# A hybrid streaming encoder layer on one core: other durations in the table that sets the emission order

## The chip, the core and the metric

The kernel runs on one core of one Trainium2 chip. The metric is the device time of one execution in microseconds (us). TensorE is written PE, its weight loads PEld, VectorE DVE, ScalarE ACT, GpSimd POOL and SyncE SP. PE's granted clock stands in the profile as a share of full speed; its two levels are 2.4 and 1.2 GHz.

## The reference

One layer of a trunk is applied to a prompt of 1024 frames and to a sample of 32 frames with carried state, all in float32, width 1024. The kernel treats the two as one sequence of 1056 columns wherever it can.

```python
h = rmsnorm(x, ln_mix_g)
z = h @ w_in + b_in                       # 1024 -> 2952 columns, split among three head groups
y_a = mLSTM(q_a, k_a, v_a, i, f)          # 4 heads of 96, chunkwise recurrence, gated and normed
y_b = stick_breaking(q_b, k_b, v_b)       # 6 heads of 64, causal, a product scan along the keys
y_c = glu(s5(u))                          # 16 groups, diagonal complex state of 64
x = x + concat[y_a, y_b, y_c] @ w_out
x = x + cross_attn(rmsnorm(x), mem_k, mem_v, w_xq, w_xo)   # 4 heads of 256, 256 memory tokens
f = (silu(causal_conv3(h2 @ w_ffn_a)) * (h2 @ w_ffn_b)) @ w_ffn_down   # h2 = rmsnorm(x), width 2816
y = rmsnorm(x + f, ln_f_g)
```

The memory keys and values of the prompt (`rmsnorm(mem_prompt) @ w_xk`, `@ w_xv`), the new states and the keys and values of the layer are outputs as well.

## The kernel before

**Dense products.** Activations lie transposed (features on partitions, frames along the free axis). A float32 product is made of three products of a high and a low part: for each block of 128 features PE runs `w_hi*h_hi`, `w_hi*h_lo` and `w_lo*h_hi` into one PSUM bank of the pool `mm`. `WStream` reads 128 columns of a weight at a time (512 KB, two buffers `w_raw`), ACT rounds them into `w_hi`, DVE subtracts for `w_lo`. Frames go in three chunks: 384, 384 and 288 columns in the input projection, 352 each later. The feed-forward part works on blocks of 264 columns.

**Stages.** The main stream runs the input projection, the memory keys and values ("kv"), `w_out` for three chunks, `xq` and `xo` of the cross attention interleaved, the two feed-forward projections, `down`, and the last norm. Beside it run *sides*, Python generators that each emit one step and then yield: `s5` with `glu`, `stick` (48 units of 128 queries, each of score matmuls, two sigmoids on ACT, a scan on DVE, a product on DVE or, up to 512 keys, on POOL, transposes on PE, and the product with the values), `mlstm` (a prelude on the gates, then nine chunks), `head` of the cross attention, norms and loads. `mlstm` starts when `s5` and `glu` are done; its chunks start when the input projection is done; `w_out` for chunk 0 waits for `stick`, `s5` and the first mLSTM chunks.

**The planner.** The order in which instructions are emitted is worked out while the program is built, by a model inside the kernel. Every engine is wrapped in `Timed`; each call asks `cost` for a duration, `operands` for the time at which its operands are there (with the latencies `LAT` between engines and DMA), and `place` puts it on that engine's time line, into a gap of the last 15 us (`REORDER`) where it fits. The main stream's own clock `clk["pe"]` is the end of its last matmul. After every second feature block, that is after six matmuls, `group` pauses and `advance` lets each side emit its next step, if that step's inputs are ready by the planner:

```python
def run(self):                                  # Side.run, shortened
    if self.done or self.ready > clk["pe"]:
        return
    ...
        self.ready = chain[0] + 0.05 - self.slack
```

`until` raises `clk["pe"]` by 0.25 us at a time where the main stream has to wait for a side. DMAs are priced in `timed` itself, 0.5 us of issue, 0.65 us and bytes over 360 GB/s. Tiles in SBUF (`Mem`, `Bag`) and PSUM (`rot`: two banks `mm`, three `gp`, three `tp`) are handed out in the order of emission. The program that this gives goes to the tile framework with `schedule_with_timeline_sim=True`. All engine calls pass through one helper, so the profile shows one line (L173) for all of them, and instructions are told apart by tile names; `za`, `zb`, `zr`, `zf`, `zy` and so on are the large memory zones.

Of the kernel before, what the change touches and what calls it, by code (L numbers as in the profile page):

```python
# [7 lines left out]
F32 = mybir.dt.float32  # L8
# [45 lines left out]
def tile_fn(tc, *args):  # L54
# [33 lines left out]
    def width(x):  # L88
        n = 1
        for d in x.shape[1:]:  # L90
            n *= d
        return n
# [39 lines left out]
    class Timed:  # L132
# [3 lines left out]
        def cost(self, name, out, ins_, args, kw):  # L136
            n = width(out)
            if self.key == "pe":
                if name == "transpose":
                    return 0.003 + 0.000834 * n  # L140
                slow = args[2].dtype == F32
                return 0.003 + n * (0.001667 if slow else 0.000417)
            if self.key == "act":
                c = 0.1 + 0.00083 * n + 0.09 * (len(ins_) - 1)
                if tabs.get(args[2], tab[0]) != tab[0]:
                    tab[0] = tabs[args[2]]
                    c += 1.28
                return c
            if self.key == "pool":
                if kw.get("op") == ALU.pow:  # L150
                    return 0.3 + 0.165 * n
                return 0.15 + n * {"memset": 0.00084, "tensor_copy": 0.0033}.get(name, 0.0021)
            per = {"reciprocal": 0.0063, "tensor_scalar": 0.0007, "tensor_copy": 0.0009, "memset": 0.0009}.get(name, 0.00105)
            return 0.08 + per * (width(ins_[0]) if name == "tensor_reduce" else n)

        def __getattr__(self, name):
            f = getattr(self.eng, name)
# [2352 lines left out]
```

## Time and profile before

| | |
|---|---|
| median of 3 runs | 1724.47 us (1716.87 to 1728.94) |
| the profiled execution | 1717.52 us, of it a span of 1715.7 us |
| mean granted PE clock | 0.987 |
| PE busy | 1639.6 us (96%) |
| PEld busy | 1595.5 us (93%) |
| DVE busy | 1137.6 us (66%) |
| ACT busy | 754.9 us (44%) |
| POOL busy | 456.2 us (27%) |
| moved by DMA | 229.90 MB, mean 134 GB/s |

The span is the time from the first to the last instruction. Busy times count an engine's instructions alone. The ends of matmuls are modelled and overlap, so a single matmul's duration is longer than the distance from one to the next; the distance is read from a run of many.

### The profile page before, as it was taken

What the parts mean: (1) busy time and instruction counts of PE and PEld (TensorE: products, weight loads), DVE (VectorE), ACT (ScalarE), POOL (GpSimd) and SP (SyncE); (2) the same over time, 40 slices, a digit from 0 to 9 for tenths busy, and PEclk for the clock granted to TensorE, in tenths of its full rate; (3) what the DMA queues carried; (4) which work ended last, traced back from release to release, by engine and by line L of the source; (5) the groups of instructions that cost most, each with busy time, mean ns of one, the idle gap of its engine ahead of it and who ended that gap; (6) DMA issues with size and microseconds to landing.
All of it is one profiled execution on the core that took longest, in us unless ns stands there. A gap on an engine that the chain in (4) does not pass through costs nothing.

```text
span 1715.7 us, 30436 instructions
## 1 busy us (share of the span) xinstructions
PE 1639.6 (96%) x11616; PEld 1595.5 (93%) x11616; DVE 1137.6 (66%) x2221; ACT 754.9 (44%) x1480; POOL 456.2 (27%) x612
## 2 busy tenths in 40 slices
PE   5999999999999899999999889999999999999997
PEld 5999989998899799999998889999999998999997
DVE  6788878745786657766656678877777777233232
ACT  5434534634665554544444534444444445111143
POOL 5234425011213333201102554333333330000022
PEclk9999999999999999999999989999999999999999
DMA  7464544254579874456653555322222227332111
GB/s 216 145 179 109 128 109 106 77 157 136 142 231 268 235 226 136 139 160 183 182 162 112 156 156 160 98 88 81 75 76 75 76 74 259 96 100 75 45 67 65
DMA packets 328391, 229.90 MB, mean 134 GB/s; under 512 B 43564, under 2 KB 309707, under 8 KB 327991
## 3 DMA queue, kind: packets, MB, share of 16 engines
q1 hardware_dynamic: 309991, 214.57, 42.6%
q10 hardware_dynamic: 18256, 13.40, 2.7%
q8 instruction: 92, 1.51, 0.4%
q14 instruction: 52, 0.43, 0.1%
HBM read 170.95 MB, written 56.38 MB: 133 GB/s over the span
## 4 chain that ended last, share of the span: by engine, by line
PE 76%; DVE 9%; DMA 9%; ACT 2%; issue 2%; POOL 2%; SPq 1%; ACTq 0%; DVEq 0%; POOLq 0%
PE mm L173 47%; PE gp L173 19%; PE tp L173 10%; DVE zy L173 3%; DVE zf L173 2%; DVE zx L173 2%; DMA out_dram<-zf 2%; DVE zr L173 1%; DVE w_lo L173 1%; POOL zf L173 1%; DMA zf<-d_act 1%; SPq L173 1%; POOL zy L173 1%; DMA d_mv<-zr 1%; DMA zf<-d_e 1%
## 5 line engine op out<-in xcount | busy, mean ns | idle before, releaser
L173 PE MATMUL mm<-zb,w_hi 128*128 128x352 f32 (+4 forms) x1234 | 365.2, 329 | 2.7 <-DVE zb L173 1.3
L173 PE MATMUL mm<-zr,w_hi 128*128 128x352 f32 (+2 forms) x1358 | 289.9, 313 | 6.3 <-DVE zx L173 2.8
L173 ACT ACTIVATE w_hi<-w_raw 128x1024 fp32r<-128x1024 f32 (+1 forms) x150 | 149.6, 997 | 284.8 <-PE mm L173 203.8
L173 PE MATMUL mm<-zb,w_lo 128*128 128x384 f32 (+2 forms) x826 | 272.4, 330 | 0.0
L173 POOL TENSOR_TENSOR zf<-zf 128x352 f32<-128x352 f32 (+5 forms) x98 | 117.4, 1200 | 578.4 <-ACT zf L173 493.2
L173 PE MATMUL mm<-zr,w_lo 128*128 128x264 f32 (+2 forms) x1058 | 236.2, 304 | 0.7 <-ACT zf L173 0.7
L173 PEld LDWEIGHTS mm<-zb,w_hi 128*128 128x128 f32 x1234 | 226.4, 189 | 4.7 <-DVE zb L173 1.6
L173 PEld LDWEIGHTS mm<-zr,w_hi 128*128 128x128 f32 x1358 | 217.2, 192 | 8.3 <-DVE zx L173 3.1
L173 DVE TENSOR_TENSOR w_lo<-w_raw,w_hi 128x1024 fp32r<-128x1024 f32 (+1 forms) x127 | 160.4, 1263 | 54.9 <-ACT w_hi L173 54.2
L173 DVE TENSOR_TENSOR zx<-mm,zx 128x352 f32<-128x352 f32 (+3 forms) x120 | 62.7, 523 | 186.1 <-PE mm L173 184.3
L173 PE MATMUL mm<-za,w_hi 128*128 128x384 f32 (+1 forms) x552 | 183.1, 332 | 0.0
L173 PEld LDWEIGHTS mm<-zr,w_lo 128*128 128x128 f32 x1058 | 164.7, 189 | 0.9 <-ACT zf L173 0.9
L173 PEld LDWEIGHTS mm<-zb,w_lo 128*128 128x128 f32 x826 | 156.5, 190 | 0.7
L173 PE MATMUL tp<-ident,zf 128*128 128x128 f32 (+3 forms) x530 | 89.2, 286 | 28.6 <-DVE zf L173 20.6
L173 PE MATMUL mm<-zy,w_hi 128*128 128x352 f32 x456 | 113.1, 324 | 1.6 <-DVE zx L173 1.6
L173 PE MATMUL gp<-zy 128*128 128x132 f32 (+13 forms) x722 | 109.8, 290 | 3.1 <-DVE zg L173 2.4
L173 DVE TENSOR_TENSOR zy<-zy 128x16 f32<-128x16 f32 (+9 forms) x371 | 97.3, 303 | 16.3 <-POOL zy L173 7.7
L173 ACT ACTIVATE zf<-gp 128x512 f32<-128x512 f32 (+6 forms) x180 | 75.6, 476 | 73.9 <-PE gp L173 57.1
L173 PEld LDWEIGHTS mm<-za,w_hi 128*128 128x128 f32 x552 | 105.6, 191 | 0.5
L173 PEld LDWEIGHTS gp<-zy 128*128 128x128 f32 (+6 forms) x722 | 97.3, 186 | 5.4 <-DVE zg L173 2.6
L173 PEld LDWEIGHTS tp<-ident,zf 128*128 128x128 f32 (+3 forms) x530 | 64.7, 146 | 38.2 <-DVE zf L173 19.2
L173 POOL TENSOR_TENSOR zy<-zy 128x16 f32<-128x16 f32 (+8 forms) x123 | 82.5, 682 | 64.4 <-DVE zy L173 54.6
(232 smaller groups left out, 3358.7 us busy)
## 6 DMA issues: line engine op xcount, KB each, us to landing
w_raw<-in_w_ffn_a_dram SPq DMA_DIRECT2D x27, 512.0 KB
w_raw<-in_w_out_dram SPq DMA_DIRECT2D x24, 512.0 KB
w_raw<-in_w_xq_dram SPq DMA_DIRECT2D x24, 512.0 KB
w_raw<-in_w_xo_dram SPq DMA_DIRECT2D x24, 512.0 KB
w_raw<-in_w_in_dram SPq DMA_DIRECT2D x23, 512.0 KB
d_act<-zx SPq DMA_DIRECT2D x22, 528.0 KB
zf<-d_act SPq DMA_DIRECT2D x22, 528.0 KB
w_raw<-in_w_ffn_down_dram SPq DMA_DIRECT2D x16, 512.0 KB
```

Source lines behind the costliest of these rows:

```text
L173: return f(*args, **kw)
```

## The change

Only the function `cost` is edited, which gives the planner its durations in us (`n` is the number of elements along the free axis). A float32r or bfloat16 matmul goes from 0.003 + 0.000417n to 0.013 + 0.000417n with a floor of 0.109, a float32 one likewise with a floor of 0.216. An ACT instruction goes from 0.1 + 0.00083n, and 0.09 for each operand beyond the first, to 0.17 + 0.00087n, and 0.19 where it also accumulates. The fixed part of a DVE instruction goes from 0.08 to 0.15, a scan doubles per element, and a copy takes the general 0.00105 in place of 0.0009. PE transposes, POOL, DMA, the latencies, the slacks and the pauses stay. The instructions are the same; the order in which they are emitted, and with it which buffer each takes, follows from the new numbers.

```diff
             if self.key == "pe":
                 if name == "transpose":
                     return 0.003 + 0.000834 * n
-                slow = args[2].dtype == F32
-                return 0.003 + n * (0.001667 if slow else 0.000417)
+                if args[2].dtype == F32:
+                    return max(0.216, 0.013 + n * 0.001667)
+                return max(0.109, 0.013 + n * 0.000417)
             if self.key == "act":
-                c = 0.1 + 0.00083 * n + 0.09 * (len(ins_) - 1)
+                c = 0.17 + 0.00087 * n + (0.19 if "accum_out" in kw else 0.0)
                 if tabs.get(args[2], tab[0]) != tab[0]:
                     tab[0] = tabs[args[2]]
                     c += 1.28
...
-            per = {"reciprocal": 0.0063, "tensor_scalar": 0.0007, "tensor_copy": 0.0009, "memset": 0.0009}.get(name, 0.00105)
-            return 0.08 + per * (width(ins_[0]) if name == "tensor_reduce" else n)
+            per = {"reciprocal": 0.0063, "tensor_scalar": 0.0007, "memset": 0.0009,
+                   "tensor_tensor_scan": 0.0021}.get(name, 0.00105)
+            return 0.15 + per * (width(ins_[0]) if name == "tensor_reduce" else n)
```

## Rows read from the trace of the kernel before

**Rows 1.** The page: busy times, and the span in 40 slices.

```profile
PE 1639.6 (96%) x11616; PEld 1595.5 (93%) x11616; DVE 1137.6 (66%) x2221; ACT 754.9 (44%) x1480; POOL 456.2 (27%) x612
...
PE   5999999999999899999999889999999999999997
...
PEclk9999999999999999999999989999999999999999
```

**Rows 2.** Busy time of each engine by stretch, clock, DMA share, GB/s.

```profile
50.00:401.00 351.00, 344.24 (x2353) 329.14 (x2352) 267.15 (x706) 156.67 (x322) 108.61 (x211) 1.00 0.48 129
401.00:475.00 74.00, 67.02 (x448) 60.62 (x447) 51.22 (x76) 45.53 (x90) 15.71 (x25) 0.95 0.55 152
475.00:594.00 119.00, 110.00 (x900) 105.35 (x899) 88.50 (x168) 71.48 (x201) 33.61 (x37) 0.95 0.87 245
594.00:650.00 56.00, 50.85 (x337) 48.74 (x338) 35.61 (x53) 30.02 (x64) 20.47 (x14) 1.00 0.70 211
650.00:930.00 280.00, 279.32 (x1819) 272.47 (x1819) 179.71 (x394) 128.88 (x258) 41.77 (x33) 1.00 0.52 156
930.00:1100.00 170.00, 153.58 (x1158) 150.50 (x1157) 134.45 (x215) 76.27 (x138) 83.64 (x79) 0.97 0.48 147
1100.00:1400.00 300.00, 300.00 (x2468) 300.00 (x2467) 231.07 (x384) 127.23 (x235) 101.54 (x133) 1.00 0.26 77
1400.00:1700.00 300.00, 295.89 (x1912) 293.70 (x1912) 117.33 (x177) 86.78 (x119) 26.33 (x30) 0.99 0.31 99
```

**Rows 3.** PE's waits from 50 to 1100 us: total us, times, longest.

```profile
PE gp L173 <- ACT w_hi L173: 6.6, 1, 6.6
PE tp L173 <- DVE zf L173: 6.6, 5, 2.9
PE tp L173 <- ACT zf L173: 4.3, 2, 2.2
PE tp L173 <- POOL zf L173: 3.6, 2, 2.0
...
PE gp L173 <- DVE zr L173: 0.5, 1, 0.5
PE mm L173 <- ACT zr L173: 0.2, 1, 0.2
```

**Rows 4.** Chain of waits in order of time: start, us, what.

```profile
543.14 5.76 DMA out_dram<-zf
...
719.98 3.87 PE mm L173 x24
...
1098.13 2.92 PE tp L173 x24
```

**Rows 5.** DVE groups by form: count, busy us, mean ns, idle before.

```profile
L173 DVE TENSOR_TENSOR zr<-tp,zr 128x512 fp32r<-128x512 f32 x40 | 26.8, 679 | 4.3 <-ACT zr L173 4.2
...
L173 DVE TENSOR_TENSOR zy<-zy 128x16 f32<-128x16 f32 x161 | 22.7, 182 | 2.8 <-POOL zy L173 1.4 <-ACT zy L173 0.6
...
L173 DVE TENSOR_TENSOR_SCAN zf<-zf 128x1024 f32<-128x1024 f32 x6 | 13.7, 2282 | 1.0 <-ACT zf L173 1.0
```

**Rows 6.** ACT groups by form.

```profile
L173 ACT ACTIVATE w_hi<-w_raw 128x1024 fp32r<-128x1024 f32 x127 | 134.6, 1060 | 240.1 <-PE mm L173 187.0 <-issue 30.5 <-DMA w_raw<-in_w_out_dram 7.7
L173 ACT ACTIVATE zf<-gp 128x512 f32<-128x512 f32 x72 | 39.7, 609 | 12.4 <-PE gp L173 8.9 <-POOL zf L173 2.3 <-DMA d_ys<-zy 1.0
```

**Rows 7.** DVE's largest group from 64 to 465 us, forms merged.

```profile
L173 DVE TENSOR_TENSOR zy<-zy 128x16 f32<-128x16 f32 (+9 forms) x333 | 88.9, 309 | 9.8 <-PE tp L173 3.0 <-ACT zy L173 2.7 <-POOL zy L173 2.2
```

**Rows 8.** PE in order of time: mLSTM prelude's last transpose, input projection's last matmul.

```profile
456.13 0.20 PE L173 MATMUL tp<-ident,zy 4*96 4x4 f32 x1
...
464.94 0.29 PE L173 MATMUL mm<-zb,w_lo 128*128 128x288 f32 x1
```

**Rows 9.** Waits of SP's DMA queue from 475 to 594 us.

```profile
SPq L173 <- DVE zf L173: 31.3, 14, 10.8
```

## The prediction

> **What bounds the kernel now.** I read the page's busy times and slices first [rows 1]: PE is busy 96% of the span, DVE 66%, ACT 44%, and PE's slices stand at 8 or 9 but for the first and the last. No instruction is added or removed, so the change can win only time in which PE does nothing, or runs slowly. The table of stretches says where that is [rows 2]. From 650 to 930, 1100 to 1400 and 1400 to 1700 us PE idles 0.7, 0.0 and 4.1 us: 880 us, half of the span, have nothing to give. The rest idles 351.0 - 344.2 = 6.8, then 7.0, 9.0 and 5.1 us up to 650 (end of the input projection, the kv stage, the first `w_out`), and 16.4 us from 930 to 1100 (the change to the feed-forward part). With 0.7 us between 650 and 930 that makes 45 us. The granted clock is below full in three of these stretches, 0.95 over 74 and 119 us and 0.97 over 170 us: (74 + 119) x 0.05 + 170 x 0.03 = 14.8 us more. The ceiling of any reordering is thus near 60 us, 3.5%; start and end of the span, where inputs come in and results go out, are left as they are.
>
> Then PE's waits between 50 and 1100 us [rows 3], which total 44.4 us. Ten kinds end with DVE (6.6 us down to 0.5, the last shown), 19.6 us; five end with ACT other than on `w_hi` (4.3 down to 0.2), 9.7 us. These 29.3 us depend on the durations that the table corrects. The single wait of 6.6 us on `w_hi` is the first half of a weight sum of the feed-forward part: a load, two POOL sums and a rounding that the code emits at a fixed point of the main stream; it stays. POOL ends 5.9 us, a DMA 1.8 and issue 0.8; their prices stay.
>
> **The change part by part.** What counts is not a price but its ratio to the main stream's clock: a side's step is emitted at the first pause at which `clk["pe"]` has passed its ready time.
>
> *The main stream.* 24 matmuls of 352 columns take 3.87 us, 161 ns each, 24 of 264 take 2.92 us, 122 ns [rows 4]. The old table says 149.8 and 113.1 ns, the new 159.8 and 123.1. So one pause (six matmuls) is 0.90 us in the old plan, 0.96 in the new, 0.97 on the chip. A table whose matmuls alone grew would only emit every step earlier; the sides' prices grow with it.
>
> The Trainium skill has a rule that speaks against this part: its page "TensorE: Matmul & The Clock Gate", section "Back-to-back issue gap", gives N/2.4 + 2.5 ns from one warm matmul to the next, 149.2 ns for 352 columns, which is the old price. The trace disagrees, with 161 ns. By the page the new table would put the main stream 7% too slow and sides too early against it, and I would put the whole change at no gain; by the row it is a correction, and the sum below stands.
>
> *An ordinary step: one ACT and one DVE instruction of 512.* Old 0.525 + 0.618 = 1.14 us, new 0.615 + 0.688 = 1.30, measured 0.609 + 0.679 = 1.29 [rows 5, 6]. In pauses: 1.27, 1.36, 1.33. A step that moves by 0.09 of a pause is emitted at another pause in one case of eleven. The rounding of a weight, 1024 wide, goes from 0.95 to 1.06 (measured 1.06) but is tied to the main stream's tiles and moves nowhere. Of the 22.7 us of waits beyond the stick's transposes, one eleventh is 2 us, and its sign is open since banks and buffers then go to other takers. I take 0; bounds a third of it either way, -7 to +7.
>
> *The stick's scans.* The scan over 1024 is priced 1.16 us before, 2.30 after, and takes 2.28 [rows 5]: from 1.3 pauses to 2.4. This is the one large error that goes. Its victims are the transposes that follow scan and product: PE waits 6.6 us in 5 waits of `tp` for DVE's `zf`, and 3.6 us in 2 for POOL's, whose product stands behind the same scan [rows 3]. Emitted a pause later, these transposes find their operand and six main matmuls run in between. Two thirds of 10.2 us, since POOL's own price stays short: -7. Bounds 0 and -10.2.
>
> *Small DVE steps in `s5`.* 161 instructions of 16 elements take 182 ns, priced 97 before and 167 after [rows 5]. `s5` with `glu` and the mLSTM prelude is a chain of such steps, and the prelude's last transpose comes 8.8 us before the last matmul of the input projection [rows 8]. Such steps and wider ones of `zy` on `zy`, nearly all of that chain, are 333 between 64 and 465 us [rows 7]: 333 x 0.07 = 23 us of price; with its copies, scans and ACT I estimate the chain 23 to 40 us longer in the plan. The main stream beside it, these 401 us, gets 7% longer, 28 us. The chain slips by -5 to +12 us against it. Only what exceeds the cover of 8.8 us reaches the mLSTM chunks: 0, at most +3 us; then the kv matmuls are next in line.
>
> *What is moved past queues.* Stores and loads of a step go with it on SP. DMA and POOL prices are unchanged while the main stream's grow 7%, so steps that wait for a load come up to 7% earlier against the matmuls: a load of 4 us, a quarter of a pause. In most of the span DMA has room (0.25 to 0.55 busy) and I cost that at nothing; the kv stage at 0.87 and 245 GB/s has none [rows 2], and there it is the second rival, 0 to +24 us.
>
> *Clock.* Idle and lowered clock fall into the same stretches, so I charge 14.8 us in proportion to the 44.4 us of waits: 7/44.4 x 14.8 = 2.3, taken as -2; bounds -10 and +5.
>
> Sum: 0 - 7 + 0 + 0 - 2 = -9 us, from 1717.5 of the profiled execution to 1708.5. That execution is 7.0 us below the median of the runs; carried over, the median goes from 1724.5 to 1715.5, half a per cent, below what a measurement of this kernel can tell from no change (about 1%, 17 us: its three runs alone span 12).
>
> **The rivals.** (a) *The order is repaired all over.* With DVE and ACT right, half to all of the 29.3 us of waits go, with their share of the clock (29.3/44.4 x 14.8 = 9.8): -20 to -39, the middle 1695 us. For it: these waits are just those that too early a transpose makes. Against: an ordinary step hardly moves, and the kv stage's waits for ACT `zf` stand behind stores that take 5.76 us each [rows 4], which no price of ACT mends.
>
> (b) *SP's queue in the kv stage.* SP issues in order; a store that waits for its DVE copy holds back the weight load behind it. In 119 us SP already waits 31.3 us in 14 waits for DVE's `zf`, 2.2 us each [rows 9]. Steps fed by loads now come earlier against the main stream, and their stores with them. The stage has 16 weight tiles of 512 KB; if each comes half such a wait later than PE wants it, that is 16 x 1.12 = 18 us and 6 us of clock, +24: 1748 us. It decides once the waits use up the lead of the second `w_raw` buffer, one tile of 24 matmuls, some 3 us; the longest is already 10.8. Against: none of PE's waits in this stage is on a weight; the one of 6.6 us comes after 930 us.
>
> (c) *The order hardly changes on the engines.* Emission is not yet an engine's queue: the framework's scheduler sorts once more, and ready main matmuls fill in for a late transpose either way. Then nothing moves: 1724 us. For it: PE already loses only 6.8 us from 50 to 401 us, where most of the stick and all of `s5` run under the wrong prices.
>
> **How the numbers follow.** The forecast gets 0.50, (a) 0.15, (b) 0.20, (c) 0.15. Faster by over 1% means under 1707: all of (a) and a fifth of the forecast, where its bounds reach low, 0.25. Slower by over 1%, above 1742: nine tenths of (b), 0.18. Within 1%: 0.57. The range goes from 1692 (the forecast's bounds summed, -27 and a little of the runs' spread; it also takes in the middle of (a)) to 1748 (b); the lower part of (a) and what lies beyond (b) stay out.
>
> **What would show it.** Right: fewer and shorter waits of `tp` for `zf` on DVE and POOL between 100 and 510 us, the same dense stretches, PE idle from 401 to 650 us at some 15 in place of 21 us. (a) would show a clock of 1.00 in the kv stage; (b) waits of PE for `w_hi` or `w_lo` between 475 and 594 us and a longer kv stage; (c) the same waits with the same totals. The forecast fails if a buffer goes to another taker and a stage starts late, most likely where `w_out` waits for three sides at once, or if `s5` slips past the input projection by more than its cover.

## The result and the profile after

The changed kernel takes 1770.41 us (median of 4 runs, 1765.79 to 1775.45) where the kernel before, timed beside it, takes 1721.12: a ratio of 1.0288, 95% interval 1.0259 to 1.0318. It is slower by 49 us, outside the predicted range of 1692 to 1748. The profiled executions, 1771.12 and 1717.52 us, differ by 53.6.

The page after, the lines of [rows 1]:

```profile
PE 1672.3 (95%) x11616; PEld 1622.8 (92%) x11616; DVE 1137.3 (64%) x2221; ACT 755.5 (43%) x1478; POOL 444.4 (25%) x612
...
PE   5999999999889798999999879999999998999998
...
PEclk9999999998889797999999999999999999999999
```

DVE works 1137.3 us against 1137.6 before, ACT 755.5 against 754.9: the same work. What differs stands in slices 10 to 16 of the PE clock, some 400 to 710 us.

By stretches, as [rows 2], with the same borders up to 650 us and the later ones moved by 54:

```profile
50.00:401.00 351.00, 339.52 (x2297) 324.37 (x2296) 262.45 (x690) 154.25 (x313) 102.14 (x203) 0.99 0.48 130
401.00:475.00 74.00, 73.07 (x463) 65.71 (x461) 41.00 (x69) 33.22 (x72) 10.82 (x24) 0.93 0.35 99
475.00:594.00 119.00, 102.79 (x770) 96.87 (x771) 83.66 (x135) 71.96 (x158) 22.58 (x30) 0.87 0.78 224
594.00:650.00 56.00, 48.59 (x300) 45.81 (x298) 29.06 (x60) 24.73 (x79) 18.80 (x21) 0.79 0.58 141
650.00:760.00 110.00, 99.27 (x580) 95.79 (x579) 67.82 (x109) 48.69 (x96) 30.77 (x28) 0.89 0.57 161
760.00:984.00 224.00, 223.99 (x1474) 217.59 (x1473) 138.76 (x335) 98.99 (x212) 23.96 (x18) 1.00 0.54 162
984.00:1154.00 170.00, 151.39 (x1136) 148.44 (x1137) 133.92 (x212) 77.26 (x139) 83.22 (x79) 0.96 0.47 144
1154.00:1454.00 300.00, 300.00 (x2469) 300.00 (x2468) 231.19 (x385) 127.01 (x235) 101.24 (x132) 1.00 0.26 77
```

From 760 us on the stretches are those of before [rows 2], 54 us later. The wait on `w_hi` in the feed-forward part marks it exactly. PE in order of time, before and then after:

```profile
1000.48 0.59 PE L173 MATMUL gp<-zr,w_hi 128*128 128x264 f32 x1 [6.65 <-ACT w_hi L173]
```

```profile
1054.68 0.59 PE L175 MATMUL gp<-zr,w_hi 128*128 128x264 f32 x1 [6.64 <-ACT w_hi L175]
```

From there to the end of the span it is 715.2 us before and 714.6 after. The last result of `w_out` is added by DVE at 702.22 us before and at 754.04 after:

```profile
702.22 0.53 DVE L173 TENSOR_TENSOR zx<-mm,zx 128x352 f32<-128x352 f32 x1 [1.33 <-PE mm L173]
```

```profile
754.04 0.53 DVE L175 TENSOR_TENSOR zx<-mm,zx 128x352 f32<-128x352 f32 x1 [0.48 <-PE mm L175]
```

That is 52 of the 54 us. The input projection ends 4 us late (below), so some 48 us of the loss lie between its end and the end of `w_out`. In the traces of all the runs below, what follows the last result of `w_out` takes 1010 to 1015 us, so no run loses anything behind it.

Between 401 and 760 us PE idles 0.9 + 16.2 + 7.4 + 10.7 = 35 us after; before, 7.0 + 9.0 + 5.1 in the first three stretches [rows 2] and nothing from 650 to 760, 21 us. The larger part is the clock. These 359 us before and after:

```profile
401.00:760.00 359.00, 337.87 (x2391) 324.57 (x2391) 249.68 (x431) 200.65 (x448) 89.61 (x93) 0.97 0.66 190
```

```profile
401.00:760.00 359.00, 323.72 (x2108) 304.19 (x2107) 221.54 (x371) 178.60 (x402) 82.98 (x100) 0.88 0.59 166
```

The clock takes (1 - 0.88) x 359 = 43 us after and 11 before, 32 more, against 14 us more of idle time. Over the whole span it is (1 - 0.966) x 1769.3 = 60 us after and (1 - 0.987) x 1715.7 = 22 before.

What came late is the mLSTM. The two rows of [rows 8] after:

```profile
469.22 0.30 PE L175 MATMUL mm<-zb,w_lo 128*128 128x288 f32 x1
...
546.84 0.21 PE L175 MATMUL tp<-ident,zy 4*96 4x4 f32 x1
```

The input projection ends 4 us later than before (464.94), the mLSTM prelude 91 us later (456.13). Its nine chunks then run for the most part behind the kv stage, whose last matmul starts at 585 us, with no other dense work beside them than `w_out`. The chain of waits after, in that part (start, us, what):

```profile
579.91 5.81 DMA d_ya<-zy
585.78 2.65 DMA zy<-d_uu
...
607.31 5.74 DMA d_ya<-zy
...
629.80 4.06 DMA d_ya<-zy
633.92 5.78 DMA zy<-d_uu
...
652.63 3.60 DMA d_ya<-zy
656.25 7.03 DMA zy<-d_uu
```

A chunk stores its result (`d_ya`) from the buffer into which a later chunk then loads its decay rows (`d_uu`); there are three such buffers. The chain runs through these stores and loads, which take some 35 of its 140 us between 550 and 690 us. The length of the nine chunks is not fixed by them: from the first score matmul to the last state product it is 112 us before, 129 after, and between 94 (e3) and 141 (e11) in the runs below. `w_out` for its chunks 1 and 2 waits for all nine. From its last result for chunk 0 to its first for chunk 1 it is 5 us before and 20 after:

```profile
635.28 0.51 DVE L173 TENSOR_TENSOR zx<-mm,zx 128x352 f32<-128x352 f32 x1
640.02 0.52 DVE L173 TENSOR_TENSOR zx<-mm,zx 128x352 f32<-128x352 f32 x1 [0.22 <-PE mm L173]
```

```profile
669.96 0.52 DVE L175 TENSOR_TENSOR zx<-mm,zx 128x352 f32<-128x352 f32 x1
689.78 0.52 DVE L175 TENSOR_TENSOR zx<-mm,zx 128x352 f32<-128x352 f32 x1
```

### The profile page after: what moved, and what is told of

Its sections match the earlier page's. It is cut to its first block, busy times and chain, and to the rows that moved or that the text cites. A ratio compares the mean times of both kernels' runs of the same rounds, so it can differ in the third digit from the quotient of the medians.

```text
span 1769.3 us, 30471 instructions
## 1 busy us (share of the span) xinstructions
PE 1672.3 (95%) x11616; PEld 1622.8 (92%) x11616; DVE 1137.3 (64%) x2221; ACT 755.5 (43%) x1478; POOL 444.4 (25%) x612
## 4 chain that ended last, share of the span: by engine, by line
PE 75%; DMA 10%; DVE 8%; ACT 3%; issue 2%; POOL 1%; SPq 0%; DVEq 0%; POOLq 0%; ACTq 0%
PE mm L175 47%; PE gp L175 18%; PE tp L175 9%; DVE zy L175 3%; DVE zf L175 2%; DVE zx L175 2%; DMA d_ya<-zy 1%; DVE zr L175 1%; DMA zy<-d_uu 1%; ACT zy L175 1%; DMA w_raw<-in_w_out_dram 1%; POOL zy L175 1%; DMA zf<-d_act 1%; DVE w_lo L175 1%; POOL zf L175 1%
## 5 line engine op out<-in xcount | busy, mean ns | idle before, releaser
L175 PE MATMUL mm<-zb,w_hi 128*128 128x352 f32 (+3 forms) x1298 | 387.7, 334 | 5.2 <-DVE zb L175 2.4
L175 PE MATMUL mm<-zr,w_hi 128*128 128x352 f32 (+2 forms) x1294 | 276.8, 315 | 12.8 <-ACT zr L175 4.8
L175 PE MATMUL mm<-zb,w_lo 128*128 128x384 f32 (+4 forms) x858 | 283.4, 330 | 0.0
L175 PEld LDWEIGHTS mm<-zb,w_hi 128*128 128x128 f32 x1298 | 241.6, 192 | 9.7 <-DVE zb L175 3.6
L175 PEld LDWEIGHTS mm<-zr,w_hi 128*128 128x128 f32 x1294 | 207.6, 193 | 15.3 <-ACT zr L175 5.4
L175 PEld LDWEIGHTS mm<-zb,w_lo 128*128 128x128 f32 x858 | 163.9, 191 | 0.7
L175 PE MATMUL tp<-ident,zf 128*128 128x128 f32 (+5 forms) x566 | 94.6, 287 | 25.2 <-DVE zf L175 14.6
L175 PEld LDWEIGHTS tp<-ident,zf 128*128 128x128 f32 (+5 forms) x566 | 69.3, 148 | 35.4 <-DVE zf L175 13.4
L175 PE MATMUL gp<-zy 128*128 128x132 f32 (+9 forms) x586 | 92.6, 296 | 0.8 <-ACT zf L175 0.7
L175 PEld LDWEIGHTS mm<-zy,w_hi 128*128 128x128 f32 x456 | 80.8, 191 | 5.1 <-ACT zr L175 4.6
```

The lines of the kernel that those rows point to most:

```text
L175: return f(*args, **kw)
```

## The experiments

Sixteen kernels, each timed in three rounds beside the kernel before; what a run loses is counted against the kernel before as it was timed beside that run. The table has for each the ratio, and from its trace, in us from the span's start: the last PE instruction of the mLSTM prelude, the last matmul of the input projection, the last of the kv stage, and the last state product of the mLSTM chunks (the row of matmuls `128*96 128x97`).

```
run                     median  ratio  95% interval      prelude input kv  chunks
before                                                       456   465 578  605
after                   1770.4  1.0288 1.0259-1.0318         547   469 585  680
e1_prelude_held         1747.3  1.0168 1.0141-1.0195         531   463 564  648
e2_dve_prices_alone     1764.2  1.0262 1.0243-1.0280         560   458 563  669
e3_pe_act_prices_alone  1763.7  1.0259 1.0239-1.0280         444   483 633  639
e4_s5_slack_1           1737.2  1.0101 1.0084-1.0119         486   462 596  623
e5_pe_prices_alone      1741.9  1.0122 1.0091-1.0153         429   478 602  619
e6_act_prices_alone     1736.7  1.0082 1.0061-1.0102         484   474 592  621
e7_dve_tenth            1742.8  1.0124 1.0093-1.0155         468   478 602  633
e8_pe_percent           1734.9  1.0067 1.0048-1.0086         479   478 590  609
e9_after_dve_157        1749.3  1.0143 1.0109-1.0177         526   474 586  654
e10_after_act_177       1746.8  1.0124 1.0092-1.0156         530   480 594  646
e11_after_dve_143       1766.0  1.0250 1.0217-1.0284         545   471 584  681
e12_pe_percent_held     1749.4  1.0142 1.0109-1.0175         530   471 564  652
e13_scan_price_alone    1731.1  1.0066 1.0049-1.0083         474   472 585  610
e14_dve_fixed_alone     1733.0  1.0078 1.0061-1.0095         511   467 582  637
e15_new_table_tuned_a   1743.0  1.0131 1.0116-1.0146         507   477 591  642
e16_new_table_tuned_b   1740.3  1.0116 1.0093-1.0140         512   468 601  633
```

The first four test theory L (the late prelude is the loss) against rivals Q (SP's queue, rival (b) of the prediction) and S (any reshuffle loses).

**e1, the prelude alone held**, with the old table:

```diff
-            while "gate" not in avail or not s5_done:
+            while "gate" not in avail or not s5_done or not h_free:
```

> The kernel before with its old table; the mLSTM prelude alone is held until the input projection is done (one more condition in the while of its first step). Theory L (the loss is the late mLSTM prelude: its last transpose came 91 us later after the change, 547 against 456 us, and the median 49 us, 0.55 us per us of slip): the prelude starts at some 465 us instead of 401 and ends at 510 to 525, a slip of 55 to 70 us, so 1750 to 1760 us. Rival Q (SP's queue and DMA-fed steps that come early against a dearer main stream): the table is old, no change, 1715 to 1730. Rival S (any reshuffled order loses what the slacks were chosen for): some loss, but the three w_out chunks need not be where it lies; 1735 to 1760.

Measured 1747.3, +28 us, 3 us under L's range and inside S's; the prelude ended at 531. Q, which expected no change, missed. The stretch from the kv stage to `w_out`, here before, after, and e1, shows how much PE got done in the same 285 us (the count after the busy time):

```profile
475.00:760.00 285.00, 270.85 (x1944) 263.95 (x1944) 198.47 (x356) 155.12 (x359) 73.90 (x68) 0.98 0.69 199
```

```profile
475.00:760.00 285.00, 250.65 (x1645) 238.47 (x1646) 180.54 (x303) 145.38 (x331) 72.16 (x77) 0.86 0.66 184
```

```profile
475.00:760.00 285.00, 252.88 (x1779) 244.56 (x1778) 181.92 (x324) 142.19 (x337) 66.94 (x75) 0.92 0.67 187
```

1944 matmuls before, 1645 after, 1779 with nothing but the prelude held; the clock falls with them, 0.98, 0.86, 0.92.

**e2, the DVE prices alone** (the last part of the change on the old table).

> The kernel before with the new DVE prices alone; PE and ACT prices are old. Theory L: the s5 chain is DVE's, its price grows and the main stream's does not, so the prelude ends at least as late as after the change, 540 us or later, and the time is 1765 to 1785 us. Rival Q (the PE price decides): 1715 to 1730. Rival S: 1735 to 1770.

Measured 1764.2, +45 us, the prelude at 560, 102 us behind the input projection. That is a microsecond under L's range and inside S's. The price of PE is old here, so Q falls as the whole cause.

**e3, PE and ACT prices alone** (the first two parts of the change).

> The changed kernel with the old DVE prices back; PE and ACT prices are new. Theory L: the main stream is dearer, s5 hardly, so the prelude ends before the input projection does, earlier than the 456 us of before, and the time is 1710 to 1730 us. Rival Q: the PE price stays, so does the loss, 1760 to 1775. Rival S: 1735 to 1770.

Measured 1763.7, though the prelude ended at 444, well ahead. L as the whole cause fell here; the ranges of Q and S both held this value.

**e4, the changed kernel with more slack for `s5` and `glu`:**

```diff
-SLACK = [-0.25, 1, -0.5]
+SLACK = [1, 1, -0.5]
```

> The changed kernel with the slack of s5 and glu at 1 in place of -0.25, so that each of their steps is emitted up to 1.25 us earlier against the main stream. Theory L: the prelude's last transpose comes at 480 to 500 us, a slip of 25 to 45 us against before, and 15 to 25 us of loss remain, 1735 to 1747 us. Rival Q: nothing on SP's queue is mended, 1760 to 1775. Rival S: any value from 1730 to 1780, without regard to where the prelude ends.

Measured 1737.2, 18 us over the kernel before, the prelude at 486: 31 of the 49 us come back, as L had it; S allowed any value. The stretch of e4:

```profile
475.00:760.00 285.00, 263.42 (x1892) 255.87 (x1892) 196.58 (x353) 159.58 (x373) 76.66 (x77) 0.96 0.68 192
```

1892 of 1944 matmuls are back, and the clock is at 0.96.

The next four split e3 and test S by neighbours: kernels with a price moved by so little that nothing is corrected.

**e5 and e6, the PE prices alone and the ACT prices alone.**

> The kernel before with the new PE prices alone. The run with PE and ACT prices lost 44 us although its prelude came early, so theory L (late prelude) is not the whole. Theory M (a dearer main stream by itself stretches the stages from the input projection to w_out: sides are emitted too early against it): 1750 to 1770 us. Theory L: 1715 to 1730. Theory S (any other order loses, since the order of before was picked among many by its measured time): 1730 to 1770, without a reason in the stages.

> The kernel before with the new ACT prices alone. Theory L: the prelude slips by 20 to 25 us against before and 5 to 15 us are lost, 1725 to 1735. Theory M: the main stream's price is old, 1715 to 1725. Theory S: 1730 to 1760.

1741.9 and 1736.7: each costs, PE's less than M asked for, ACT's 2 us more than L had, both inside S's ranges. Together (e3) they cost more than the sum, 44 us against 20 + 15.

**e7 and e8, two neutral neighbours of the kernel before:**

```diff
-            return 0.08 + per * (width(ins_[0]) if name == "tensor_reduce" else n)
+            return 0.087 + per * (width(ins_[0]) if name == "tensor_reduce" else n)
```

```diff
-                return 0.003 + n * (0.001667 if slow else 0.000417)
+                return 0.003 + n * (0.001667 if slow else 0.000421)
```

> The kernel before with the fixed part of a DVE instruction at 0.087 in place of 0.08, a tenth of the change and no correction worth the name. Theories L and M: the prelude and the main stream stay where they were, so 1715 to 1728 us. Theory S: another order, and 10 to 30 us lost, 1730 to 1750.

> The kernel before with the price of a float32r column at 0.000421 in place of 0.000417, one per cent. Theories L and M: 1715 to 1728 us. Theory S: 10 to 30 us lost, 1730 to 1750.

1742.8 and 1734.9: 21 and 13 us lost by changes that correct nothing. S holds for this part: the order of before is better than orders next to it.

**e9, e10, e11, three neutral neighbours of the changed kernel** (0.157 for DVE's 0.15, 0.177 for ACT's 0.17, 0.143 for DVE's 0.15), **and e12, e8 with the prelude held** as in e1.

> The changed kernel with the fixed part of a DVE instruction at 0.157 in place of 0.15: a neutral neighbour of the changed kernel, as two runs before were neighbours of the old one, which lost 13 and 21 us against it. Theory S+ (both kernels are draws: the old one a picked good one, its neighbours 1735 to 1743; the changed one a plain draw of a table that is no better and no worse): 1730 to 1755 us, on the average of the neighbours near 1742. Theory L+ (what is left above the old neighbours, some 30 us, is the late prelude, which the new table always brings): 1755 to 1780.

> The changed kernel with the fixed part of an ACT instruction at 0.177 in place of 0.17, a second neutral neighbour. Theory S+: 1730 to 1755 us. Theory L+: 1755 to 1780.

> The changed kernel with the fixed part of a DVE instruction at 0.143 in place of 0.15, a third neutral neighbour; of the three its mLSTM prelude is emitted latest against the end of the input projection, near to where the changed kernel has it. Theory S+: 1730 to 1755 us, no later than the other two. Theory L+: 1760 to 1780, the slowest of the three.

> The neighbour of the old kernel with PE's price one per cent up (1734.9 us by itself), its mLSTM prelude held until the input projection is done. Theory L+: the prelude ends 55 to 70 us later, and at the rate of the old kernel's held run (28 us) this is 1755 to 1768 us. Theory S+: the held run of the old kernel lost mainly because it left a picked order; here the order is a plain one already, and 1732 to 1748 follow.

1749.3 and 1746.8 fit S+, 1766.0 fits L+ and is, as L+ had it, the slowest of the three. e12 took 1749.4, between the two forecasts: it loses 25 us where e8 lost 13, so a plain order also pays for a held prelude, 12 us, less than half of what e1 paid. The changed kernel lies at the dear end of its neighbours, which lose 25, 22 and 42 us, and the place of the mLSTM goes with it: the chunks' last state product lies at 646 and 654 in the two quicker ones, at 681 and 680 in the two slow ones.

e1, e4 and e12 are new orders as well, and neighbours differ by up to 19 us without any reason in the prices. So neither 28 nor 31 nor 12 us is the price of the mLSTM's place alone. What these runs show is the direction: holding the prelude costs twice, moving it forward gains.

**e13 and e14, the doubled scan price alone, and DVE's fixed part with the copies alone.**

> The kernel before with the doubled price of a scan alone. The prediction had the scans as the one correction that pays. Theory L+ (what decides beyond the draw is the prelude's place, which the fixed part of DVE's many small instructions moves, not the scans): the prelude ends within 15 us of the input projection's end and the time is that of a neighbour, 1735 to 1745. The prediction's own step (scans priced right save 7 us): 1712 to 1725.

> The kernel before with DVE's fixed part at 0.15 and copies at 0.00105, scans at the old price. Theory L+: the prelude ends 30 to 60 us after the input projection, 1745 to 1765 us. If scans and fixed part only slip the prelude together: 1735 to 1745.

e13: 1731.1, just under the neighbours' band; the scans don't pay by themselves. e14: 1733.0, and L+ misses: the prelude ended 44 us after the input projection, yet the chunks ended at 637. Here the time goes with the chunks' end, not with the prelude's.

**e15 and e16, the new table with the planner's other constants chosen for it:**

```diff
-SAMPLE_AT = 2
+SAMPLE_AT = 3
...
-IN_ORDER = "b0 b1 a0 a1 b2 a2".split()
+IN_ORDER = "b0 a0 b1 b2 a1 a2".split()
...
-REORDER = 15.0
-SLACK = [-0.25, 1, -0.5]
+REORDER = 30
+SLACK = [2, -0.5, 0.75]
...
-            add(Window(heads(), 2, 2.0))
+            add(Window(heads(), 2, 1))
```

This is e15; e16 has `REORDER` 22, `SLACK` [0.75, -0.5, 0], `SAMPLE_AT` 4 and the rest as it was.

> The new table with the planner's other constants chosen for it: slacks 2, -0.5, 0.75, a window of 30 us for gaps, the sample of a head pair after unit 3, the input projection's parts as b0 a0 b1 b2 a1 a2, slack 1 for the heads of the cross attention. The new table's own plan ends at 1710 us with them, at 1775 with the old constants, and at 1768, 1757, 1756 and 1751 for four kernels that took 1766, 1749, 1747 and 1737 us. Theory S+ (the constants were chosen for the old prices; with true prices the plan tells the time, and constants chosen by it win the draw back): 1695 to 1715 us. If the plan tells nothing beyond these: 1730 to 1770.

> As the run beside it, with slacks 0.75, -0.5, 0, a window of 22 us, the sample after unit 4, the rest old; its plan ends at 1716 us. Theory S+: 1700 to 1720 us. Otherwise 1730 to 1770.

1743.0 and 1740.3: 26 and 29 us better than the changed kernel, 33 and 24 us above the times that their own plans gave, and slower than the kernel before. S+ missed. No kernel of this study beats the kernel before.

Read afterwards over all changed orders, the chunks' end puts the times into three bands: up to 637 us, 1731 to 1743; 642 to 654 us, 1743 to 1749; 669 to 681 us, 1764 to 1770. Within the first band it orders nothing: e5 takes 1742 with 619, e14 takes 1733 with 637. Only e3 falls out, 1763.7 with 639. There the kv stage itself ends at 633 us, 30 us after any other. In it ACT's copies wait 13.6 us, in 6 waits, for stores of the memory keys and values to leave their buffers (4.5 us in 3 waits before). These waits alone do not explain it, since e9 has 10.2 us of them in a kv stage no longer than before; the cause in e3 stays open.

## Why the prediction was wrong

*Two steps failed.* The first is "Small DVE steps in `s5`": "the chain slips by -5 to +12 us against it", "0, at most +3 us". The prediction named this slip as a way to fail, and the mechanism is the one at work, but the size was off by far: against the end of the input projection the prelude moved from 9 us ahead to 78 behind, 86 us. The parts of the change account for it: against that end DVE's prices move the prelude by 111 us (e2), ACT's by 19 (e6) and PE's by -41 (e5), 89 together. The prediction had 23 to 40 for the first two and -28 for the last.

I added the new prices of the chain's own steps in a row, as if the chain had DVE to itself in the plan. It shares that planned engine, above all with the stick's scans. The stretch that the prediction counted, before the change:

```profile
64.00:465.00 401.00, 390.57 (x2660) 371.25 (x2658) 300.14 (x718) 186.66 (x380) 109.56 (x215) 0.99 0.48 129
```

DVE has 718 instructions there, of which I counted 333. 718 x 0.07 = 50 us is an estimate of what the fixed part alone adds to DVE's planned queue, and alone it moved the prelude by 53 (e14). The scan price alone moved it by 11 (e13), all DVE prices by 111 (e2), more than the sum. That it is the planned queue is argued from these numbers, not isolated.

Of the slip I let only what exceeds the cover count, and did not follow the chunks to their end, where `w_out` waits. Of the 49 us, e4 gives back 31 by moving the prelude forward, and holding it in tables without the change costs 28 (e1) and 12 (e12).

The second is "An ordinary step", "I take 0", -7 to +7. It took another order as equal in the mean. Four kernels with small or single corrections of the old table (e7, e8, e13, e14) lose 11 to 21 us, 0.84% on average, and none gains. That is the size of the 18 us that e4 leaves; how the 49 us divide between the two steps is not shown more closely, since every run is also a new order. A likely reason for the second, not shown here, is that the order of before and the constants around the table were picked together under the old prices.

*The scans* were right in part: from 100 to 520 us PE's `tp` waited 6.6 us for DVE's `zf` and 3.6 for POOL's before; after the change 0.6 and 0.6. The scan price alone (e13) brings 1.9 and 4.0, and with every DVE price but the scan's (e14) it is 3.9 and none: DVE's wait falls in both and POOL's goes where the scan price is old, so the gain is not shown to be the scan price's. Other waits took their place: all of PE's waits in this stretch were 13.5 us before and are 24.1 after, led by

```profile
PE gp L175 <- ACT zf L175: 5.3, 4, 2.1
PE tp L175 <- ACT zf L175: 4.4, 1, 4.4
```

*The main stream's price*: right to a nanosecond as a duration, but a right price alone costs 20 us (e5). *Clock*: I charged it in proportion to waits, 2.3 us for 7; in fact it is some 32 us of clock against 14 of idle time between 401 and 760 us.

*The rivals.* (a) and (c) are refuted. (b) came out nearest in time (1748) but by another mechanism: in the changed kernel the waits of PE on `w_hi` and `w_lo` from 475 to 760 us come to 4.8 us, and the kv stage is 4 us longer. e5, the PE price alone, lost 20 us, close to (b)'s 24, but none of PE's waits in its kv stage is on a weight, though that stage is 14 us longer. What was right is where nothing moves: the stretches from `xq` on, the wait of 6.6 us, and the 715 us behind it.

## What to carry to other kernels

In this kernel truer durations did not make a better plan while the planner's other constants stayed as they were. Choosing those again by the new plan won back 26 and 29 of the 49 us and no more, and both picked settings fell short of their plans, by 33 and 24 us. So measure several neutral neighbours of a version before judging it, and do not compare one draw with one picked order. When a side feeds a later stage through a chain that ends in a wait, read when that chain starts and ends, and price everything that shares its engine in the plan, not the chain's own steps alone.

## What was not expected of the hardware

A stretch that shows PE full can still be slow, and a fall of the clock need not follow a wait. In the changed kernel PE waited 4.4 us for ACT's `zf` until 387 us; after that it was busy without a break to 426 us:

```profile
388.00:392.00 4.00, 4.00 (x15) 4.00 (x14) 1.12 (x4) 1.16 (x1) 0.00 (x0) 0.50 0.64 158
392.00:416.00 24.00, 24.00 (x156) 22.82 (x154) 9.06 (x15) 10.31 (x22) 3.35 (x5) 1.00 0.46 136
416.00:426.00 10.00, 10.00 (x41) 8.21 (x41) 1.40 (x6) 1.94 (x4) 2.50 (x5) 0.51 0.10 29
```

The first low stretch follows the wait. The second, ten microseconds at the lower of the two levels, has no wait before it; from 413.5 to 416 us PE had run mostly matmuls with one column (24 of them). In the kernel before, 24 such matmuls in a row at 374 us were followed by no fall, so the reason is not separated. The clock column has to be read beside the busy time.
